# The first quarter's norm taken from channel-major tiles by products with ones, and the filler weights' split moved up

## The chip, the cores and the metric

The kernel runs on one core of one Trainium2 chip. The metric is the device time of one execution in microseconds (us). A core has a tensor engine (PE, with its weight loads as PEld), a vector engine (DVE), a scalar engine (ACT), a GpSimd engine (POOL) and a sync engine (SP), which here issues every DMA.

## The reference

One encoder block on 1024 tokens of 1024 channels, in float32:

```python
h = rms_norm(x, norm_mix_pre[l])      # x * rsqrt(mean(x*x over channels) + 1e-6) * g
proj = h @ w_in[l]                    # 1024 -> 5376 columns
p_sb, p_rw = ...                      # columns of attention and of RWKV-7
gates = sigmoid(proj[..., SB_COLS + RW_COLS:] + b_gate[l])
o_sb = stick_breaking_attention(q, k, v)
o_rw = rwkv7_time_mix(p_rw, ...)      # has a LoRA part and a chunked recurrence
merged = gates[..., :D] * (o_sb @ w_sb_out[l]) + gates[..., D:] * (o_rw @ w_rw_out[l])
x = x + rms_norm(merged @ w_o[l], norm_mix_post[l])
h = rms_norm(x, norm_ffn_pre[l])
x = x + rms_norm((silu(h @ w_ffn_gate[l]) * (h @ w_ffn_up[l])) @ w_ffn_down[l], norm_ffn_post[l])
```

The change touches the first line and the way in which some weight tiles of `gates` are prepared.

## The kernel before, in words

Every large product is done in three passes. A float32 operand is split into a high part (a cast on ACT) and a low part (a subtraction on DVE), and the products high by high, high by low and low by high are added in PSUM. `b.split` does this for any tile, `b.parts` for a weight tile of 128 x 1024, and `b.weights` is a load followed by `b.parts`. Loaded weights lie in the tile class `raw`, their parts in the classes `whi` and `wlo`; each of these classes has two places.

The kernel doesn't issue its instructions as they are written. `Block.record` writes down each operation with its cost, its tiles and a priority, which is its number in the order of writing plus an offset. `Block.schedule` then plays the whole program through with estimated durations and writes out an order for each engine: of the operations that are ready on an engine, the one with the lowest priority number goes first. It also hands out the places of the tile classes. So each engine's order is fixed when the kernel is built, from estimates, and nearly all instructions carry line 590, where the planned operations are issued. `with b.filler()` adds 10**7 to the priority: such work goes where nothing else is ready.

The stages in order of time are: the norm of x and the LoRA part (to about 63 us in the profile), four pairs of RWKV heads (`rwkv`, to about 440 us), the attention, the gates in pairs and the merge, the output projection, and the feed-forward part.

The first stage is `norm_in`. The tokens are worked in four quarters t of TQ = 256. x is loaded twice: token-major as `b.xin[m]` (eight tiles `b_x`, 128 tokens x 1024 channels, 512 KB each) and channel-major as `b.xt[2*t+q]` (eight tiles `b_xt`, 128 channels x 4 blocks x 256 tokens, 512 KB each). `scales(t)` takes the two token tiles of a quarter: ACT squares each and sums it along the row, ACT does Ln and Exp to have one over the root of the mean, DVE multiplies the identity by that number for each token (`b_dg`), and PE multiplies a tile of ones by this diagonal, so that the number of each token stands in all 128 partitions, in a PSUM tile (`e_e` for t = 0, 1 and `c_c` for t = 2, 3). Then for each of eight channel blocks DVE multiplies the channel-major tile by the channel's gain and by this row of scales (`SCALAR_TENSOR_TENSOR b_xt<-b_xt,par_par,e_e`, 128x256), and `b.split` writes the high and low parts into `b.hT` (`big_h`). `scales(t + 1)` is written down in the middle of quarter t.

`weights(i)` splits the two LoRA weight tiles (`b.w_lora`): the high part by a cast on POOL (`POOL CAST b_b<-raw_raw`), the low part by a subtraction on DVE (`TENSOR_TENSOR b_b<-raw_raw,b_b`). The LoRA products are the matmuls `d_d<-big_h,b_b` and `y_y<-big_h,b_b` of 256 columns, 192 of them.

The loads are issued by SP in the order written: token tile 0, the identity (`cst`), token tile 1, `par`, LoRA weight 0, the two channel tiles of t = 0, LoRA weight 1, token tiles 2 and 3, the channel tiles of t = 1, and so on.

`idle_products` are bf16 matmuls on zeros whose result nobody reads: nine at the start (`AWAKE[0]`), and eight (`AWAKE[1]`) that come after the last ones-product of the first quarter.

`gate_tiles` computes gate columns as filler: one weight tile is loaded and split, 48 matmuls of 512 columns follow in two halves of the tokens, ACT copies each half out of PSUM, and SP stores it (`gsc`). One such tile is written down in the first RWKV pair, one in the third, and two in the last part of the attention:

```python
GATES_R = (1, 0, 1, 0)
ATT_GATES = {(3, 0): 1, (3, 4): 1}
SINGLE = (8, 12, 9, 13)
```

Of the kernel before, what the change touches and what calls it, by code (L numbers as in the profile page):

```python
# [6 lines left out]
F32 = mybir.dt.float32  # L7
F32R = mybir.dt.float32r
BF16 = mybir.dt.bfloat16
AF = mybir.ActivationFunctionType  # L10
ALU = mybir.AluOpType
# [4 lines left out]
P = 128  # L16
S = 1024
D = 1024
KT = D // P
# [17 lines left out]
AWAKE = (9, 8)  # L37
TQ = S // 4
# [219 lines left out]
}  # L258
MARGIN = 80
CHAIN = -1000  # L260


def wait(e, to):
# [391 lines left out]
def hybrid_block(tc, x, xt, w_in, consts, params, rows, ups, gup, w_sb, w_rw, w_o, w_fg, w_fu, w_fd, out):  # L655
    b = Block(tc, {a.tensor.name for a in (x, xt, w_in, consts, params, rows, ups, gup, w_sb, w_rw, w_o, w_fg, w_fu, w_fd)})
    nc = b
    T = b.t
    with ExitStack() as es:
        b.open(es)  # L660
        b.cls("cst", 1, CC_TI)
        b.cls("par", 1, PC_N)
        b.cls("small", 4, 16)
        b.cls("tiny", 4, 4)
        b.cls("ss", 8, 4)
        b.cls("carry", 5, 1)
        b.cls("pl", 3, 8)
        b.cls("sp", 3, CH)
        b.cls("q", 4, 256)
        b.cls("big", 4, 4 * S)  # L670
        for n in ("raw", "whi", "wlo"):
            b.cls(n, 2, S)
        b.cls("b", NB, 1040, halves=True)
        for n, k in (("d", 2), ("e", 2), ("c", 2), ("y", 2)):
            b.cls(n, k, H, psum=True)

        cst, par = T("cst", [P, CC_TI]), T("par", [P, PC_N])

        one = T("q", [P, P])
        nc.gpsimd.memset(one, 1.0)  # L680
        b.zero = T("b", [P, H], BF16, "zero")
        nc.vector.memset(b.zero, 0.0)
        idle_products(b, AWAKE[0])

        b.xin, b.w_lora, b.xt = [], [], []
        def tokens(*ms):
            for m in ms:
                b.xin.append(T("b", [P, D], F32, "x"))
                nc.sync.dma_start(b.xin[m], x[m * P : m * P + P, :])
        def channels(t):  # L690
            for q in range(2):
                b.xt.append(T("b", [P, 4, TQ], F32, "xt"))
                nc.sync.dma_start(b.xt[-1], xt[t][:, 4 * q : 4 * q + 4, :])
        tokens(0)
        nc.sync.dma_start(cst[:, 0:P], consts[:, 0:P])
        tokens(1)
        nc.sync.dma_start(par, params)
        b.w_lora.append(b.load(w_in[24], [P, KT, P]))
        channels(0)
        b.w_lora.append(b.load(w_in[25], [P, KT, P]))  # L700
        tokens(2, 3)
        channels(1)
        tokens(4, 5)
        nc.sync.dma_start(cst[:, P:CC_TI], consts[:, P:CC_TI])
        channels(2)
        tokens(6, 7)
        channels(3)
        b.ident = cst[:, CC_ID : CC_ID + P]
        b.cen = cst[:, CC_CEN : CC_CEN + P]
        b.ones = cst[:, CC_ONE : CC_ONE + P]  # L710
        b.mask_a = cst[:, CC_MA : CC_MA + P]
        b.tinit = consts[:, CC_TI : CC_TI + 256]
        b.scanm = consts[:, CC_SC:CC_N]
        b.eps = T("small", [P, 2])
        nc.gpsimd.memset(b.eps[:, 0:1], RMS_EPS)
        nc.gpsimd.memset(b.eps[:, 1:2], GN_EPS)
        b.om = T("small", [P, 14])
        nc.gpsimd.tensor_scalar(out=b.om, in0=par[:, PC_MU : PC_MU + 14], scalar1=-1.0, scalar2=1.0, op0=ALU.mult, op1=ALU.add)
        b.oka = T("small", [P, 4])
        nc.gpsimd.tensor_scalar(out=b.oka, in0=par[:, PC_KA : PC_KA + 4], scalar1=-1.0, scalar2=1.0, op0=ALU.mult, op1=ALU.add)  # L720
        b.pc = lambda col: par[:, col : col + 1]

        b.gsc = [b.scratch([P, S], f"gsc{j}") for j in range(16)]
        b.orw_d = [b.scratch([P, S], f"orw{p}") for p in range(PAIRS)]
        b.x2_d = b.scratch([S, D], "x2d")
        b.w_in, b.w_sb, b.w_rw = w_in, w_sb, w_rw
        b.ngate = 0

        b.h_d = [b.scratch([4, P, S], f"h_d{q}") for q in range(2)]
        b.steady = STEADY[0]  # L730
        norm_in(b, one)
        lora(b, ups, gup)
        b.steady = STEADY[1]
        rwkv(b)
        b.steady = STEADY[2]
        attention(b)
        b.steady = STEADY[3]
        ms, sums = merge(b)
        b.steady = True
        output(b, x, w_o, rows, ms, sums)  # L740
        ffn(b, w_fg, w_fu, w_fd, rows, out)
        b.issue()


def idle_products(b, n, after=None):
    ps = b.t("y", [P, H])
    for i in range(n):
        b.tensor.matmul(ps, lhsT=b.zero[:, 0:P], rhs=b.zero, start=True, stop=True)
        if after:
            b.ops[-1].preds.add(after)  # L750


def norm_in(b, one):

    nc = b.nc
    T = b.t
    b.hT = tuple([T("big", [P, 4, S], F32R, "h") for q in range(2)] for i in range(2))
    b.table("natural_log_exp_and_others")
    ss = T("small", [P, 16])
    rs = []  # L760

    def scales(t):
        if t % 2 == 0:
            rs.append(T("ec"[t // 2], [P, 4, P]))
        dg = T("b", [P, 2, P], F32, "dg")
        for i in range(2):
            m = 2 * t + i
            nc.scalar.activation(b.xin[m], b.xin[m], AF.Square, accum_out=ss[:, m : m + 1])
        r = ss[:, 8 + 2 * t : 10 + 2 * t]
        nc.scalar.activation(r, ss[:, 2 * t : 2 * t + 2], AF.Ln, scale=1.0 / D, bias=b.eps[:, 0:1])  # L770
        nc.scalar.activation(r, r, AF.Exp, scale=-0.5)
        for i in range(2):
            nc.vector.tensor_scalar(out=dg[:, i], in0=b.ident, scalar1=r[:, i : i + 1], scalar2=None, op0=ALU.mult)
            nc.tensor.matmul(rs[t // 2][:, 2 * (t % 2) + i, :], lhsT=one, rhs=dg[:, i], start=True, stop=True)

    def weights(i):
        w = b.w_lora[i]
        hi, lo = T("b", [P, KT, P], F32R), T("b", [P, KT, P], F32R)
        nc.gpsimd.tensor_copy(hi, w)
        nc.vector.tensor_tensor(out=lo, in0=w, in1=hi, op=ALU.subtract)  # L780
        b.w_lora[i] = hi, lo

    scales(0)
    idle_products(b, AWAKE[1], b.ops[-1])
    weights(0)
    for t in range(4):
        r = rs[t // 2].rearrange("p i t -> p (i t)")[:, t % 2 * TQ : t % 2 * TQ + TQ]
        ts = slice(t * TQ, t * TQ + TQ)
        for q in range(2):
            h = b.xt[2 * t + q]  # L790
            for k in range(4):
                nc.vector.scalar_tensor_tensor(out=h[:, k], in0=h[:, k], scalar=b.pc(PC_G + 4 * q + k), in1=r, op0=ALU.mult, op1=ALU.mult)
                if k % 2:
                    ks = slice(k - 1, k + 1)
                    b.split(b.hT[0][q][:, ks, ts], b.hT[1][q][:, ks, ts], h[:, ks])
            with Offset(b, 500):
                nc.sync.dma_start(b.h_d[q][:, :, ts].rearrange("k p t -> p k t"), h)
            if t < 3 and q == 0:
                scales(t + 1)
            if t == 0 and q == 0:  # L800
                weights(1)


def gate_tiles(b, n):
    nc = b.nc
    with b.filler():
        for j in SINGLE[b.ngate : b.ngate + n]:
            w = b.weights(b.w_in[26 + j], [P, KT, P])
            for hf in range(2):
                ps = b.proj(w, hf)  # L810
                g = b.t("b", [P, H], F32, "g")
                nc.scalar.copy(g, ps)
                nc.sync.dma_start(b.gsc[j][:, hf * H : hf * H + H], g)
    b.ngate += n
# [173 lines left out]
def rwkv(b):  # L988
# [15 lines left out]
    for p in range(PAIRS):  # L1004
# [10 lines left out]
        if p == PAIRS - 1:  # L1015
            b.table("sigmoid_and_others")
        with Offset(b, CHAIN):
            for hf in range(2):
# [444 lines left out]
def output(b, x, w_o, rows, ms, sums):  # L1463
# [104 lines left out]
    product(Z, 3, True, False, third)  # L1568
    with Offset(b, CHAIN):
        for m in range(4):  # L1570
# [7 lines left out]
def ffn(b, w_fg, w_fu, w_fd, rows, out):  # L1578
    b.act = b.scratch([7, NFF // 2, P, H], "act")
    ffn_up(b, w_fg, w_fu)  # L1580
    ffn_down(b, w_fd, rows, out)
# [21 lines left out]
def ffn_up(b, w_fg, w_fu):  # L1603
# [38 lines left out]
    def first(r1, cls="d"):  # L1642
# [3 lines left out]
        e1 = T("b", [P, H], F32, "u")  # L1646
        with Offset(b, CHAIN):
            nc.scalar.copy(e1, pa)
# [4 lines left out]
    for g in range(LEAD):  # L1653
        e1, c11 = [], []
        for w in (w_fg, w_fu):
            e, pa = first(b.load(w[g], [P, KT, P]), "de"[w is w_fu])
            e1.append(e)
            c11.append(T("b", [P, H], F32, "u"))
            with Offset(b, CHAIN):
                nc.scalar.copy(c11[-1], pa)  # L1660
# [255 lines left out]
```

## Time and profile before

| | |
|---|---|
| median of three runs | 1575.42 us (1575.28 to 1575.59) |
| profiled execution, its own time | 1575.67 us |
| its span in the trace | 1573.9 us |
| PE busy | 1544.2 us, 98% of the span |
| PEld busy | 1248.3 us, 79% |
| DVE busy | 1201.3 us, 76% |
| ACT busy | 766.7 us, 49% |
| POOL busy | 203.7 us, 13% |
| DMA | 201.35 MB, mean 128 GB/s |

The span is counted from the first instruction of the trace. A row of the timeline reads: start, duration, engine, line, operation, out<-in, shapes, how many, and in brackets how long the engine was idle before it and what released it. In the table of stretches, each engine has its busy time and, in brackets, its instructions. A matmul's recorded duration is longer than its share of PE's time, because matmuls overlap.

### The profile page before, as it was taken

Reading aid. Unit: us, or ns where it says so; the run is one execution under the profiler, and the core shown is the slowest. Engines: PE = TensorE matmul, PEld = TensorE weight load, DVE = VectorE, ACT = ScalarE, POOL = GpSimd, SP = SyncE. Lnnn points to the kernel's source line nnn. Section 1 sums busy time; section 2 is a strip of 40 time slices with the busy share of each in tenths; the row PEclk is TensorE's granted clock in tenths of the full one; section 3 lists DMA queues with packets and bytes.
Section 4 is the critical chain, followed back from the end, with each engine's and each line's share of the span. In section 5 each row is a group of like instructions: output and inputs, shape, how many; then the busy total and the mean of one; then the engine's idle time right before and its main releaser. Section 6 shows DMA issues by size and latency. Waiting matters only on the chain.

```text
span 1573.9 us, 23740 instructions
## 1 busy us (share of the span) xinstructions
PE 1544.2 (98%) x8733; PEld 1248.3 (79%) x8733; DVE 1201.3 (76%) x2046; ACT 766.7 (49%) x1527; POOL 203.7 (13%) x383
## 2 busy tenths in 40 slices
PE   7999999999999999999999999999999999999998
PEld 6877777777887888788888887888888888888886
DVE  7769898987687979766379797778766766877575
ACT  6734453545577767523446696332323323454352
POOL 1132354444413220000000000000000000000000
PEclk9999999999999999999999999999999999999999
DMA  9723342322010003445632543334322323964543
GB/s 368 278 82 90 88 102 71 100 74 55 28 41 28 27 28 128 154 132 171 219 120 95 170 154 106 115 126 141 120 88 100 114 88 140 336 219 141 193 155 134
DMA packets 116949, 201.35 MB, mean 128 GB/s; under 512 B 43104, under 2 KB 48480, under 8 KB 116832
## 3 DMA queue, kind: packets, MB, share of 16 engines
q1 hardware_dynamic: 116832, 199.83, 38.0%
q8 instruction: 69, 1.13, 0.3%
q14 instruction: 48, 0.39, 0.1%
HBM read 146.05 MB, written 51.64 MB: 126 GB/s over the span
## 4 chain that ended last, share of the span: by engine, by line
PE 78%; DVE 10%; issue 3%; DMA 3%; ACT 3%; POOL 1%; SPq 0%; DVEq 0%; POOLq 0%; ACTq 0%
PE d_d L590 28%; PE e_e L590 20%; PE c_c L590 19%; PE y_y L590 12%; DVE q_q L590 1%; DVE b_sh L590 1%; DMA b_nl<-nd 1%; DVE b_nx L590 1%; DVE b_tmp L590 1%; POOL sp_sp L590 1%; ACT b_qst L590 1%; DVE b_nb L590 1%; DMA raw_raw<-w_fu 1%; DMA h_d<-b_xt 1%; DVE b_sv L590 1%
## 5 line engine op out<-in xcount | busy, mean ns | idle before, releaser
L590 PE MATMUL d_d<-big_h,whi_whi 128*128 128x512 f32 x896 | 308.7, 411 | 0.9 <-DVE b_sh L590 0.9
L590 PEld LDWEIGHTS d_d<-big_h,whi_whi 128*128 128x128 f32 x896 | 163.7, 189 | 33.3 <-issue 4.1
L590 PE MATMUL d_d<-big_h,wlo_wlo 128*128 128x512 f32 x448 | 184.9, 413 | 0.1
L590 PEld LDWEIGHTS d_d<-big_h,wlo_wlo 128*128 128x128 f32 x448 | 84.6, 189 | 16.2 <-issue 1.7
L590 DVE TENSOR_TENSOR_SCAN b_nb<-b_nb 128x128 f32<-128x128 f32 (+3 forms) x64 | 86.1, 1360 | 4.4 <-POOL b_nb L590 3.9
L590 POOL TENSOR_SCALAR sp_sp<-b_sv,pl_pl 64x64 f32<-64x64 f32 x120 | 66.8, 557 | 77.7 <-DVE b_sv L590 71.4
L590 ACT CAST whi_whi<-raw_raw 128x1024 fp32r<-128x1024 f32 (+1 forms) x44 | 39.2, 892 | 67.7 <-PE d_d L590 58.7
L590 PE MATMUL d_d<-b_wd,big_act 128*128 128x512 f32 x264 | 66.4, 394 | 0.0
L590 PE MATMUL e_e<-b_wd,big_act 128*128 128x512 f32 x264 | 66.3, 393 | 0.0
L590 PE MATMUL e_e<-big_h,whi_a 128*128 128x512 f32 x252 | 63.6, 395 | 0.0
L590 PE MATMUL e_e<-big_h,b_a 128*128 128x512 f32 x240 | 59.6, 394 | 0.0
L590 DVE TENSOR_TENSOR b_wd<-b_wraw,b_wd 128x512 fp32r<-128x512 f32 x65 | 42.5, 686 | 21.3 <-ACT b_wd L590 21.2
L590 PEld LDWEIGHTS d_d<-b_wd,big_act 128*128 128x128 f32 x264 | 49.6, 188 | 11.6
L590 PEld LDWEIGHTS e_e<-b_wd,big_act 128*128 128x128 f32 x264 | 49.6, 188 | 11.5
L590 PE MATMUL e_e<-big_h,wlo_a 128*128 128x512 f32 x228 | 56.3, 395 | 0.5 <-ACT b_mg L590 0.5
L590 ACT CAST b_wd<-b_wraw 128x512 fp32r<-128x512 f32 x65 | 38.6, 619 | 37.1 <-DVE b_wraw L590 14.5
L590 PEld LDWEIGHTS e_e<-big_h,whi_a 128*128 128x128 f32 x252 | 47.2, 188 | 11.0
L590 DVE TENSOR_TENSOR wlo_wlo<-raw_raw,whi_whi 128x1024 fp32r<-128x1024 f32 (+1 forms) x44 | 45.3, 1029 | 12.8 <-ACT whi_whi L590 12.7
L590 DVE TENSOR_TENSOR b_wt<-c_c,b_wt 128x512 fp32r<-128x512 f32 (+2 forms) x96 | 50.1, 546 | 4.6 <-ACT b_wt L590 3.9
L590 PEld LDWEIGHTS e_e<-big_h,b_a 128*128 128x128 f32 x240 | 45.1, 188 | 10.5
L590 PEld LDWEIGHTS e_e<-big_h,wlo_a 128*128 128x128 f32 x228 | 42.7, 188 | 11.0 <-ACT b_mg L590 1.0
L590 PE MATMUL d_d<-big_h,b_a 128*128 128x512 f32 x204 | 51.1, 395 | 0.1
(733 smaller groups left out, 3837.8 us busy)
## 6 DMA issues: line engine op xcount, KB each, us to landing
raw_raw<-w_in SPq DMA_DIRECT2D x48, 512.0 KB, 3.7
raw_raw<-w_fg SPq DMA_DIRECT2D x27, 512.0 KB, 3.5
raw_raw<-w_fu SPq DMA_DIRECT2D x27, 512.0 KB, 3.5
b_wraw<-w_fd SPq DMA_DIRECT2D x22, 512.0 KB, 5.2
act<-b_u SPq DMA_DIRECT2D x37, 256.0 KB, 2.2
b_x<-x SPq DMA_DIRECT2D x16, 512.0 KB, 5.8
b_mg<-gsc SPq DMA_DIRECT2D x30, 256.0 KB, 5.3
raw_araw<-act SPq DMA_DIRECT2D x14, 512.0 KB, 4.5
```

The costliest lines, as they stand in the source:

```text
L590: getattr(getattr(self.real, op.engine), op.method)(**kw)
```

## The change

Four things are done.

1. The loads of token tiles 0 and 1 are left out. The two channel-major tiles of t = 0 are loaded first, then `par`, LoRA weight 0, the identity, LoRA weight 1, and the rest as before.
2. For t = 0, `scales` gives way to `first_scales`. ACT squares the first channel-major tile, and four products by ones, of 256 columns in float32, add the squares over the 128 channels of a block. DVE squares the second tile, adds its halves, and two more products by ones follow into the same PSUM tile. Then ACT does Ln and Exp on 128 x 256 elements and writes the row of scales `r0` into SBUF, from where DVE's multiplications read it.
3. The eight idle products now come after the last of these six products.
4. In `gate_tiles`, the load keeps its filler priority, but the split of the weight tile is given the offset `SOON`, which takes the filler's 10**7 off again: the split competes by its place in the order of writing.

```diff
+SOON = -(10**7)
...
-        tokens(0)
-        nc.sync.dma_start(cst[:, 0:P], consts[:, 0:P])
-        tokens(1)
+        channels(0)
         nc.sync.dma_start(par, params)
         b.w_lora.append(b.load(w_in[24], [P, KT, P]))
-        channels(0)
+        nc.sync.dma_start(cst[:, 0:P], consts[:, 0:P])
         b.w_lora.append(b.load(w_in[25], [P, KT, P]))
         tokens(2, 3)
         channels(1)
...
     def scales(t):
-        if t % 2 == 0:
+        if t < 3:
             rs.append(T("ec"[t // 2], [P, 4, P]))
...
-    scales(0)
-    idle_products(b, AWAKE[1], b.ops[-1])
+    def first_scales():
+        ps = T("e", [P, TQ])
+        squares = [T("b", [P, 4, TQ], F32, "sq") for q in range(2)]
+        nc.scalar.activation(squares[0], b.xt[0], AF.Square)
+        for k in range(4):
+            nc.tensor.matmul(ps, lhsT=one, rhs=squares[0][:, k], start=k == 0, stop=False)
+        nc.vector.tensor_tensor(out=squares[1], in0=b.xt[1], in1=b.xt[1], op=ALU.mult)
+        nc.vector.tensor_tensor(out=squares[1][:, 0:2], in0=squares[1][:, 0:2], in1=squares[1][:, 2:4], op=ALU.add)
+        for k in range(2):
+            nc.tensor.matmul(ps, lhsT=one, rhs=squares[1][:, k], start=False, stop=k == 1)
+        r = T("b", [P, TQ], F32, "r0")
+        nc.scalar.activation(r, ps, AF.Ln, scale=1.0 / D, bias=b.eps[:, 0:1])
+        nc.scalar.activation(r, r, AF.Exp, scale=-0.5)
+        return r
+
+    r0 = first_scales()
+    idle_products(b, AWAKE[1], next(op for op in reversed(b.ops) if op.engine == "tensor"))
     weights(0)
     for t in range(4):
-        r = rs[t // 2].rearrange("p i t -> p (i t)")[:, t % 2 * TQ : t % 2 * TQ + TQ]
+        r = rs[t // 2].rearrange("p i t -> p (i t)")[:, t % 2 * TQ : t % 2 * TQ + TQ] if t else r0
...
         for j in SINGLE[b.ngate : b.ngate + n]:
-            w = b.weights(b.w_in[26 + j], [P, KT, P])
+            raw = b.load(b.w_in[26 + j], [P, KT, P])
+            with Offset(b, SOON):
+                w = b.parts(raw, [P, KT, P])
```

More of the change, by code (lines that the diff above doesn't have):

```diff
@@ L683, in hybrid_block @@
         idle_products(b, AWAKE[0])
-        b.xin, b.w_lora, b.xt = [], [], []
+        b.xin, b.w_lora, b.xt = {}, [], []
         def tokens(*ms):
             for m in ms:
-                b.xin.append(T("b", [P, D], F32, "x"))
+                b.xin[m] = T("b", [P, D], F32, "x")
                 nc.sync.dma_start(b.xin[m], x[m * P : m * P + P, :])
```

## The prediction

> **What bounds the kernel now.** I read the head of the page first, then a table of stretches of the whole run, which shows where PE stands still.
>
> ```profile
> span 1573.9 us, 23740 instructions
> PE 1544.2 (98%) x8733; PEld 1248.3 (79%) x8733; DVE 1201.3 (76%) x2046; ACT 766.7 (49%) x1527; POOL 203.7 (13%) x383
> ```
>
> ```profile
> 0.00:11.33 11.33, 5.25 (x14) 2.30 (x15) 1.53 (x3) 4.08 (x7) 2.90 (x12) 1.00 0.82 293
> 11.33:16.34 5.01, 3.62 (x10) 1.28 (x8) 5.01 (x9) 2.39 (x4) 1.04 (x1) 1.00 1.02 403
> 16.34:44.00 27.66, 26.59 (x206) 24.90 (x206) 25.97 (x54) 23.17 (x43) 1.79 (x7) 1.00 0.88 336
> 44.00:140.00 96.00, 95.97 (x465) 75.72 (x466) 70.36 (x120) 45.50 (x74) 18.75 (x44) 1.00 0.50 168
> 140.00:440.00 300.00, 290.79 (x2841) 227.71 (x2840) 257.80 (x596) 152.38 (x356) 135.31 (x249) 1.00 0.28 74
> 440.00:640.00 200.00, 198.22 (x1190) 169.06 (x1189) 174.49 (x256) 145.30 (x328) 43.87 (x70) 1.00 0.17 56
> 980.00:1560.00 580.00, 580.00 (x2506) 470.25 (x2505) 409.22 (x625) 211.99 (x353) 0.00 (x0) 1.00 0.43 148
> ```
>
> The columns are the stretch and its length, then busy time and instructions of PE, PEld, DVE, ACT and POOL, the granted clock, and the share and rate of the DMA. PE is the bound: it idles 29.7 us of 1573.9. What a change of order can gain is in those 29.7 us, because the change takes no product out of the later stages. They lie in three places that matter here: 7.5 us before 16.34 (6.08 + 1.39), 1.1 us from there to 44, and 9.2 us in the RWKV stretch from 140 to 440. The attention stretch has 1.8 us, and from 44 to 140 PE doesn't idle, so a head start gained by 44 is kept at least until 140.
>
> The third view is the timeline of the first stage. It shows that DVE is the feeder there.
>
> ```profile
> 4.05 1.06 ACT L590 ACTIVATE b_x<-b_x 128x1024 f32<-128x1024 f32 x1 [2.03 <-DMA b_x<-x]
> 7.08 1.06 ACT L590 ACTIVATE b_x<-b_x 128x1024 f32<-128x1024 f32 x1 [1.89 <-DMA b_x<-x]
> 8.90 1.25 DVE L590 TENSOR_SCALAR b_dg<-cst_cst,small_small 128x128 f32<-128x128 f32 x2 [7.76 <-ACT small_small L590]
> 10.10 1.19 PE L590 MATMUL e_e<-b_dg,q_q 128*128 128x128 f32 x4 [4.89 <-DVE b_dg L590]
> 11.09 3.36 PE L590 MATMUL y_y<-b_zero 128*128 128x512 bf16 x8
> 11.33 2.05 DVE L590 SCALAR_TENSOR_TENSOR b_xt<-b_xt,par_par,e_e 128x256 f32<-128x256 f32 x5 [1.18 <-PE e_e L590]
> 12.97 1.04 POOL L590 CAST b_b<-raw_raw 128x1024 fp32r<-128x1024 f32 x1 [3.10 <-DMA raw_raw<-w_in]
> 13.30 1.86 DVE L590 TENSOR_TENSOR big_h<-b_xt,big_h 128x512 fp32r<-128x512 f32 x2
> 15.08 1.21 DVE L590 TENSOR_TENSOR b_b<-raw_raw,b_b 128x1024 fp32r<-128x1024 f32 x1
> 16.34 4.02 PE L590 MATMUL d_d<-big_h,b_b 128*128 128x256 f32 x26 [1.35 <-DVE b_b L590]
> 20.20 0.61 PE L590 MATMUL e_e<-b_dg,q_q 128*128 128x128 f32 x4
> 20.85 2.83 DVE L590 SCALAR_TENSOR_TENSOR b_xt<-b_xt,par_par,e_e 128x256 f32<-128x256 f32 x7 [0.65 <-PE e_e L590]
> 27.93 2.05 DVE L590 SCALAR_TENSOR_TENSOR b_xt<-b_xt,par_par,c_c 128x256 f32<-128x256 f32 x5 [0.88 <-PE c_c L590]
> ```
>
> From 11.33, when the first scales arrive, DVE is busy without a break to 16.34 and for 25.97 of the 27.66 us after that. PE waits for it (1.35 us at 16.34, for the low part of the first LoRA weight). So the stage ends when DVE has worked off its list, and three things set that: when DVE may start (11.33), where it is held up, and the two waits of 0.65 and 0.88 us for the scales of the next quarters.
>
> **The change part by part, against the profiled execution's 1575.67 us** (span 1573.9 and 1.8 around it; it stands 0.25 us above the median of 1575.42).
>
> *Start of DVE's list.* Before, the second token tile let ACT start at 7.08, and the scales came to DVE at 11.33: 4.25 us later. Now the second channel tile stands where the second token tile stood, without the identity ahead of it. The first 512 KB landed by 4.05, as for a token tile. For the second I bound: not before 4.05 plus 512 KB at the 403 GB/s of the second stretch, 1.30 us, so 5.35; not after 7.08. I take 6.7, nearer to the row measured, since the LoRA weight that follows shares the engines as before. Then: DVE squares 128x1024, 1.21 us by the row at 15.08, to 7.9; DVE adds 128x512, and two products by ones follow. The normal DVE subtraction of 128x512, and the scalar engine on 128 x 256 out of PSUM, are in these rows (by tile, with shortest, median and longest; and by form, with the mean in ns behind the busy time):
>
> ```profile
> L590 DVE TENSOR_TENSOR big_h<-b_xt,big_h x16: 679/686/1255, 13.3 to 40.8; 128x512 fp32r<-128x512 f32 x16
> ```
>
> ```profile
> L590 ACT ACTIVATE b_nb<-e_e 128x256 f32<-128x256 f32 x16 | 6.3, 392 | 0.7 <-PE e_e L590 0.5
> ```
>
> The add takes 0.69, to 8.6. Two float32 products by ones of 128 columns took 0.61 us where PE had been busy (20.20) and 1.19 where it had idled for 4.89 us (10.10). With 256 columns I double: 1.2 or 2.4. PE's gap before them is here about 1.5 us (the first four products end near 7.1), nearer to no gap, so 1.2: to 9.8. Ln and Exp at 0.39 each: 10.55. DVE starts 0.8 us sooner. The ends: tile at 5.35 with fast products, 2.1 sooner; tile at 7.08 with slow products, 0.8 later. What is taken out here (ACT's two squares, two diagonals, two products) lay on this chain and is replaced whole; the first four new products and ACT's first square hide under the wait for the second tile.
>
> The Trainium skill ("TensorE: Matmul & The Clock Gate", What's actually happening) says that PE runs at half its clock by default and after an idle window of some 3.4 us, and at full clock after as long a busy one. The trace agrees that the early products are slow: the eight idle products of 512 columns took 3.36 us, 0.42 each, though the granted clock reads 1.00. By that rule the last two products run fast after a 1.5 us gap, and the sum stays; were the array still slow, it would be 1.2 us worse.
>
> *POOL beside DVE.* At 13.30 two subtractions took 1.86 where two cost 1.37; the longest of that kind, 1255 ns, lies beside POOL's cast of LoRA weight 1 at 12.97. That weight now has 1 MB less ahead of it, 2.6 us at 403 GB/s: the cast falls to about 10.4, on DVE's first multiplications. The gain of 0.5 is sure to move; I take back 0.2 for the new place: net -0.3, ends -0.5 (nothing is held) and +0.5 (a hold of the cast's whole 1.04).
>
> *Waits for the next scales.* Token tiles 2 and 3 come 2.6 us sooner by the same 1 MB. The scales of t = 1 then need not wait: I take the 0.65 out whole and, since ACT is busy 23.17 of 27.66 us by then, half of the 0.88: -1.1, ends 0 and -1.5. Late next is DVE itself.
>
> *Loads moved past others.* SP issues two loads fewer; `par` and the identity change places, and the identity is first needed by the diagonals of t = 1. Nothing: the cover is the work of quarter 0 on DVE. The eight idle products hold PE after the sum for 1.7 to 3.4 us, to at most 13.2, while the low part of LoRA weight 0 is not done before about 14: nothing.
>
> *The filler's split.* The gate weight of the first RWKV pair is one of the two casts below; its two halves leave at 145.23 and 163.40, and each cast waited for PE, that is for a place among the high parts.
>
> ```profile
> 125.67 1.07 ACT L590 CAST whi_whi<-raw_raw 128x1024 fp32r<-128x1024 f32 x1
> 135.82 1.04 ACT L590 CAST whi_whi<-raw_raw 128x1024 fp32r<-128x1024 f32 x1 [4.69 <-PE d_d L590]
> ```
>
> ```profile
> 145.23 0.34 SPq L590 DMA_DIRECT2D gsc<-b_tmp  x1
> 163.40 0.32 SPq L590 DMA_DIRECT2D gsc<-b_sh  x1
> ```
>
> ```profile
> L590 DVE TENSOR_TENSOR wlo_wlo<-raw_raw,whi_whi 128x1024 fp32r<-128x1024 f32 x14 | 17.2, 1226 | 1.5 <-ACT whi_whi L590 1.4
> L590 ACT CAST whi_whi<-raw_raw 128x1024 fp32r<-128x1024 f32 x14 | 14.7, 1047 | 19.0 <-PE d_d L590 19.0
> ```
>
> The last two rows are the 14 splits of the RWKV stretch: ACT idled 19.0 us in front of the casts for PE to free a place, not for priority. So a higher priority alone changes little: I take 0. The ends: a gain of a third of the 9.2 us that PE idles there, -3.1; a loss of one split's duration, 1.05 + 1.23 = 2.3, wherever a projection waits for a place that a filler weight holds.
>
> *A new order after the start.* All estimates behind the start shift, and the fixed orders may fall out otherwise with the same work. I take 0, ends 2 us on both sides, about a fifth of the idle time from 140 to 440.
>
> Sum: -0.8 - 0.3 - 1.1 + 0 + 0 = -2.2. From 1575.67 that is 1573.5, on the median 1573.3.
>
> **The rivals.**
>
> *The filler fills the RWKV waits* (faster). PE's longest waits in that stretch are for the chain on DVE:
>
> ```profile
> PE c_c L590 <- DVE b_sv L590: 2.2, 5, 0.8
> PE e_e L590 <- DVE b_nx L590: 1.9, 4, 0.7
> PE c_c L590 <- DVE b_xv L590: 1.8, 2, 1.2
> ```
>
> Ready gate products could fill them. Against it: the 19.0 us above, and that the row at 125.67 already lies before the first wait. With 3.1 us: 1570.2.
>
> *Given back* (same). DVE finishes sooner, but the RWKV chain, which waits for DVE and loads of its own, takes up the shift as longer PE waits. For it: 9.2 us idle in spite of filler. Against it: from 44 to 140 PE is full, so the shift does arrive. Time: 1575.4.
>
> *The cast on the multiplications* (less gained). `r0` is read from SBUF where PSUM was read before. At 12.97 the cast lay beside a multiplication with a PSUM operand and beside the subtraction, and it was the subtraction that got longer. If the multiplications are now held for the cast's 1.04 us, the sum loses 0.8: 1574.1. The Trainium skill ("GPSIMD Engine Reference", 1. Specifications) says that POOL shares its SBUF interfaces with DVE where DVE has two SBUF inputs. By that rule this hold comes. The trace agrees, with the 1255 ns.
>
> *A filler weight blocks a place* (slower). With two places, a gate weight that is split early and whose 48 products wait as filler leaves one place for the projections: each then costs a bare split of 2.3 us. Against it: during that time PE has just those filler products to do. It decides from three such stalls: 1573.3 + 6.9 = 1580.2.
>
> **How the numbers follow.** The forecast 1573.3 gets 0.46, with a range of its own of 1570.8 to 1575.5; the cast on the multiplications 0.08, given back 0.16, the filled waits 0.20, the blocked place 0.10. A measurement of this kernel can tell about 0.2% from no change: 3.15 us, so faster is below 1572.3 and slower above 1578.6. The filled waits are faster with 0.18, and 0.18 of the forecast's 0.46 lies below 1572.3: 0.36. Slower is the blocked place, 0.10. Same is the rest, 0.54. The range is 1568.8 to 1577.8: it leaves out most of the blocked place and the far tail of the filled waits.
>
> **What would show it.** Right: the first multiplication on DVE starts at 10.0 to 11.0; its list has no waits of 0.5 us for scales in quarter 1; PE's dense part starts before 15; the LoRA stage ends about 2 us sooner; PE's idle time from 140 to 440 stays within 2 us of 9.2. Wrong: the second channel tile lands after 7.1, the two last products by ones take over 2 us, or PE's idle time from 140 to 440 moves by more than the whole start gains. That last would make the time itself wrong.

## The result, and the profile after

The changed kernel takes 1564.17 us (median of 6 runs, 1563.44 to 1566.39), the one before 1575.09 (1573.91 to 1575.59): ratio 0.9934, interval 0.9922 to 0.9947. That is faster by 10.9 us; forecast were 2.2. The profiled execution took 1564.33 us with a span of 1562.5, against 1575.67 and 1573.9.

The head of the page after, and the table of stretches with the limits used before (stretch and length; busy time and instructions of PE, PEld, DVE, ACT, POOL; granted clock, DMA share and rate):

```profile
span 1562.5 us, 23763 instructions
PE 1539.6 (99%) x8741; PEld 1250.9 (80%) x8741; DVE 1204.9 (77%) x2046; ACT 765.7 (49%) x1524; POOL 209.5 (13%) x383
```

```profile
0.00:11.33 11.33, 8.26 (x29) 4.03 (x29) 3.36 (x6) 3.48 (x5) 5.25 (x13) 1.00 0.84 313
11.33:16.34 5.01, 2.67 (x12) 2.50 (x13) 5.01 (x12) 4.65 (x11) 0.00 (x0) 0.78 1.00 377
16.34:44.00 27.66, 27.66 (x212) 26.55 (x212) 27.46 (x54) 24.43 (x44) 1.84 (x6) 0.98 0.91 335
140.00:440.00 300.00, 290.79 (x2856) 230.26 (x2856) 259.21 (x591) 151.80 (x353) 137.73 (x251) 1.00 0.26 72
440.00:640.00 200.00, 199.50 (x1195) 171.18 (x1194) 180.21 (x266) 148.75 (x334) 45.96 (x68) 1.00 0.20 66
```

PE's idle time from 140 to 440 is 9.21 us, to the hundredth what it was. Yet PE ran 2856 products there in place of 2841. PE's busy column can't show that; the count of products can, and so can the busy time of the weight loads (227.71 us before, 230.26 after). The limits here are fixed and the changed kernel is some 3 us ahead, so the two stretches don't hold quite the same work; the table further down has its limits at events.

The timeline of the start after:

```profile
5.89 3.21 PE L591 MATMUL e_e<-b_sq,q_q 128*128 128x256 f32 x12 [1.26 <-ACT b_sq L591]
5.97 1.23 DVE L591 TENSOR_TENSOR b_sq<-b_xt 128x1024 f32<-128x1024 f32 x1 [4.83 <-DMA b_xt<-xt]
7.92 2.02 POOL L591 CAST b_b<-raw_raw 128x1024 fp32r<-128x1024 f32 x2
10.16 2.07 DVE L591 SCALAR_TENSOR_TENSOR b_xt<-b_xt,par_par,b_r 128x256 f32<-128x256 f32 x5 [2.24 <-ACT b_r L591]
13.29 1.28 DVE L591 TENSOR_TENSOR big_h<-b_xt,big_h 128x512 fp32r<-128x512 f32 x2
14.02 3.28 PE L591 MATMUL d_d<-big_h,b_b 128*128 128x256 f32 x14 [1.83 <-DVE big_h L591]
18.41 2.43 DVE L591 SCALAR_TENSOR_TENSOR b_xt<-b_xt,par_par,e_e 128x256 f32<-128x256 f32 x6
23.85 2.05 DVE L591 SCALAR_TENSOR_TENSOR b_xt<-b_xt,par_par,c_c 128x256 f32<-128x256 f32 x5
```

The second channel tile is there at 5.97, the first multiplication starts at 10.16 (before: 11.33). The two waits for scales (0.65 and 0.88) are both gone: the rows at 18.41 and 23.85 have no idle time in front. Both casts on POOL are over at 9.94, and two subtractions at 13.29 take 1.28 in place of 1.86.

For the rest, stretches are cut at the same events in each kernel: the first k-projection product (`d_d<-big_h,whi_whi`), the first and the last attention transpose (`c_c<-cst_cst,b_nb`), the first product of the paired gates with `b_tp`, and the first with `b_wd` (these two at their weight loads). The same columns, for the kernel before:

```profile
42.90:428.40 385.50, 376.21 (x3188) 293.98 (x3186) 319.75 (x701) 190.81 (x409) 151.84 (x288) 1.00 0.34 98
428.40:629.50 201.10, 199.32 (x1259) 170.22 (x1258) 173.62 (x254) 145.68 (x334) 46.09 (x75) 1.00 0.15 49
629.50:661.50 32.00, 30.27 (x140) 24.44 (x139) 27.16 (x45) 19.06 (x36) 0.00 (x0) 1.00 0.48 158
661.50:837.00 175.50, 175.50 (x757) 141.87 (x756) 109.75 (x171) 65.53 (x103) 0.00 (x0) 1.00 0.48 159
```

And for the changed kernel:

```profile
39.30:425.50 386.20, 376.99 (x3201) 296.93 (x3200) 322.91 (x702) 190.30 (x409) 150.73 (x289) 1.00 0.33 97
425.50:621.40 195.90, 195.41 (x1248) 168.53 (x1247) 172.96 (x253) 145.22 (x333) 51.66 (x75) 1.00 0.15 51
621.40:651.50 30.10, 30.10 (x140) 24.50 (x139) 27.13 (x45) 19.27 (x36) 0.00 (x0) 1.00 0.51 174
651.50:827.00 175.50, 175.50 (x757) 141.81 (x756) 110.48 (x172) 66.44 (x105) 0.00 (x0) 1.00 0.48 158
```

The first k-projection product comes 3.6 us sooner. The RWKV stretch is 0.7 longer, but holds 13 products more; the attention stretch is 5.2 shorter with 11 products fewer. By tile, the eleven are products of 512 columns with the split weights: with `whi_whi` there are 626 before and 634 after in the RWKV stretch, and 262 and 254 in the attention; with `wlo_wlo` 313 and 316, and 130 and 127. The other two are LoRA products that now lie behind the first k-projection product. Then 1.9 us go between 629.5 and 661.5, and nothing up to `b_wd`: 10.0 of the 11.4 us that the spans differ by lie ahead of the feed-forward part.

### The profile page after: what moved, and what is told of

It is laid out like the page before. It is cut to its first block, busy times and chain, and to the rows that moved or that the text cites. A ratio compares the mean times of both kernels' runs of the same rounds, so it can differ in the third digit from the quotient of the medians.

```text
span 1562.5 us, 23763 instructions
## 1 busy us (share of the span) xinstructions
PE 1539.6 (99%) x8741; PEld 1250.9 (80%) x8741; DVE 1204.9 (77%) x2046; ACT 765.7 (49%) x1524; POOL 209.5 (13%) x383
## 4 chain that ended last, share of the span: by engine, by line
PE 83%; DVE 10%; ACT 3%; DMA 2%; issue 1%; POOL 0%; SPq 0%; DVEq 0%; POOLq 0%; ACTq 0%
PE d_d L591 29%; PE e_e L591 22%; PE c_c L591 19%; PE y_y L591 13%; DVE q_q L591 2%; DVE b_tmp L591 1%; DVE b_sh L591 1%; DVE b_pp L591 1%; DVE b_sv L591 1%; DVE b_bk L591 1%; DVE b_nx L591 1%; ACT b_qst L591 1%; DMA q_q<-td 0%; DVE wlo_wlo L591 0%; DVE b_sg L591 0%
## 5 line engine op out<-in xcount | busy, mean ns | idle before, releaser
L591 PEld LDWEIGHTS e_e<-big_h,b_a 128*128 128x128 f32 x240 | 45.1, 188 | 10.4
```

The costliest lines, as they stand in the source:

```text
L591: getattr(getattr(self.real, op.engine), op.method)(**kw)
```

## The experiments

Three theories stood at the outset. *Head start*: what the start saves is carried to the end and is all there is. *Order*: an edit at the start changes every estimate behind it, the lists of all engines are dealt anew, and these lists are better. *Split first*: the new priority itself pays. Gains below are worked out from the ratio to the kernel before, timed beside each kernel, times 1575 us, with the 95% interval. The kernels are called by the first part of their names, `e1` to `e16`.

### The priority alone taken out, and one priority of four

`e1_norm_only` has the new norm and the old priority:

```diff
-            raw = b.load(b.w_in[26 + j], [P, KT, P])
-            with Offset(b, SOON):
-                w = b.parts(raw, [P, KT, P])
+            w = b.weights(b.w_in[26 + j], [P, KT, P])
```

> The changed kernel with the filler weights' split put back to its old priority; the new norm of the first quarter stays. The changed kernel took 1564.2 us and the one before 1575.1, so 10.9 us are to be explained. Theory 'head start' (the start is worth all of it, carried to the end): 1564 to 1565, and the split's priority is worth under 1 us. Theory 'order' (the start is worth the 3.5 us by which the first k-projection product comes sooner, the rest is the lists that fell out otherwise): the lists of this kernel are those of the changed one up to about 590 us and differ after that, so it should stand level with the changed kernel up to the last of the attention stretch and end anywhere from 1562 to 1572. Theory 'split first' (the priority itself pays): 1570 to 1572, the loss lying in the attention stretch.

`e9_last_split_first` gives it to the last weight alone:

```diff
-            with Offset(b, SOON):
+            with Offset(b, SOON if j == SINGLE[3] else 0):
```

> The changed kernel with the high priority for the split of the last filler gate weight alone (the one projected beside the last attention head); the three before it have the old priority. The lists come out instruction for instruction as the changed kernel's on all five engines, so this is also the changed kernel once more on this chip. Theory 'one split' (of the new priority only the last weight's matters): level with the changed kernel, 5 to 11 us below the kernel before, and 20 us and more below the kernel with the new norm alone. Rival 'all four matter': 3 us and more over the changed kernel. If start and order only add up, 1567 to 1570; if the changed kernel's first measurement holds on this chip, 1563 to 1566.

The first took 1589.83 us: 15.0 slower than before (12.4 to 17.3), outside what all three theories expected. The second took 1565.71, 10.2 faster (8.0 to 12.4), as the changed kernel, whose lists it has. So, given this norm, the priority of one split in four is worth 25 us; *split first* had the right stretch, with 6 to 8 us. With the old norm the same priority changes nothing: the lists come out as those of the kernel before, instruction for instruction.

The reason stands in the low parts of the filler weights on DVE, late in the attention stretch (view by tile from 555 us on: shortest, median, longest; first and last start). The kernel before, the changed one, and `e1_norm_only`:

```profile
L590 DVE TENSOR_TENSOR wlo_wlo<-raw_raw,whi_whi x2: 1190/1207/1224, 558.7 to 578.3; 128x1024 fp32r<-128x1024 f32 x2
```

```profile
L591 DVE TENSOR_TENSOR wlo_wlo<-raw_raw,whi_whi x1: 1209/1209/1209, 593.3 to 593.3; 128x1024 fp32r<-128x1024 f32 x1
```

```profile
L591 DVE TENSOR_TENSOR wlo_wlo<-raw_raw,whi_whi x1: 1219/1219/1219, 633.7 to 633.7; 128x1024 fp32r<-128x1024 f32 x1
```

With the old priority the last low part runs at 633.7, after the attention. Its 48 products, meant to fill PE's waits in the attention, then have no waits to fill, and PE stands still in both places. The timeline and the stretch of that kernel:

```profile
634.93 0.80 PE L591 MATMUL d_d<-big_h,wlo_wlo 128*128 128x512 f32 x1 [5.40 <-DVE wlo_wlo L591]
```

```profile
440.00:640.00 200.00, 186.18 (x1098) 158.71 (x1097) 177.76 (x262) 142.07 (x321) 46.14 (x69) 0.95 0.14 46
```

PE is idle for 13.8 us from 440 to 640, against 0.5 in the changed kernel, and the granted clock is 0.95 in place of 1.00.

### Start and order parted

`e2_new_norm_old_order` has the new norm and, from the LoRA products on, the kernel before's order on every engine and its places for the tiles, written out as lists; `e3_old_norm_new_order` is the converse; `e5_after_by_list` is the changed kernel with its own lists. The edit is the same in all:

```diff
-            for op in self.schedule():
+            for tile, at in zip(self.tiles, PLACES):
+                tile.where = (at // 2, at % 2, tile.small)
+            for op in (self.ops[k] for k in ORDER):
```

> The new norm of the first quarter, but from the LoRA projections on every engine runs its instructions in exactly the order of the kernel before, with every tile at the place that it had there (the order and the places are written out as a list). Theory 'head start': 1564 to 1566, since the start alone carries the gain. Theory 'order': 1571.0 to 1572.0, that is the 3.5 us that the first k-projection product came sooner and no more. Theory 'given back': 1574 to 1576.

> The converse: the old norm of the first quarter with its four token tiles, and from the LoRA projections on every engine's instructions in the order of the changed kernel, tiles at the changed kernel's places. Theory 'head start': 1574 to 1576, no gain. Theory 'order': 1567 to 1568.5, that is 7 to 7.5 us of gain with no sooner start. If both new_norm_old_order and this one gain less than their part, the order pays only together with the start.

> The changed kernel itself, its own order and places written out as a list: the same instructions in the same order on every engine. It is the measure for the kernels below and for the two mixed ones (new norm with old order: 3.3 us gained; old norm with new order: 2.7 us gained). If start and order add up and nothing else is at work, it stands about 6 us below the kernel before, at 0.996 of it; if the two pay only together, 10 to 11 us below, at 0.993, as the changed kernel did.

They gained 3.3 us (1.7 to 4.7), 2.5 (1.1 to 3.8) and 5.5 (3.5 to 7.7); the last was timed on another chip than the first two. So neither part carries the whole, and the three were run once more side by side:

> The changed kernel's order as a list, beside the two mixed kernels on one chip. It gained 5.8 us on one chip, and the changed kernel itself 9.5 on the other, on which the mixed ones gained 3.3 and 2.7. Theory 'start and order add up': its gain here is that of the two mixed kernels together, within 1.5 us. Theory 'they pay only together': its gain is larger than their sum by 3 us or more.

> The new norm with the order of the kernel before, beside the other two on one chip. Theory 'start and order add up': 2.8 to 3.5 us under the kernel before, by the 2.8 us that the first k-projection product came sooner in its profile. Theory 'they pay only together': the same, but the three don't sum.

> The old norm with the changed kernel's order, beside the other two on one chip. In its first profile it stood 5.2 us ahead at the FFN's first weight and lost 2 after that, at a granted clock of 0.97 from 920 to 980 us. Theory 'start and order add up', with the order worth 5: 5 us under the kernel before. Theory 'they pay only together': 2.7 us again.

Now 8.2 (6.1 to 10.2) for both, 3.5 (2.2 to 4.9) for the new norm alone and 3.3 (1.9 to 4.9) for the new order alone. 3.5 + 3.3 = 6.8 lies inside the first interval: start and order add up as well as this can be told, with 1.4 us left over that the intervals don't settle. Each is worth about as much as the other. *Head start* as the whole cause is out, *order* is right in kind. The stretches show what each does. New norm, old order (`e15`):

```profile
40.20:425.70 385.50, 375.79 (x3187) 294.11 (x3186) 319.15 (x701) 190.34 (x408) 150.78 (x288) 1.00 0.33 97
425.70:626.60 200.90, 199.05 (x1260) 170.16 (x1260) 173.56 (x254) 145.71 (x334) 46.33 (x75) 1.00 0.15 49
```

Old norm, new order (`e16`):

```profile
43.40:429.10 385.70, 378.11 (x3202) 296.70 (x3200) 323.20 (x701) 190.24 (x409) 150.89 (x289) 1.00 0.34 98
429.10:625.10 196.00, 195.57 (x1247) 168.34 (x1245) 172.82 (x252) 145.26 (x333) 51.78 (x75) 1.00 0.15 51
```

The norm moves the stretches and leaves them as long as before. The order moves 13 or so products from the attention, where PE idles 1.8 us in 201, into the RWKV stretch, which takes them at no visible cost of time (385.5 to 386.2 us in these four profiles, with 3187 or with 3202 products). One execution differs from another by more than that: in the profile of `e14`, with the changed kernel's lists, the stretch took 388.6 us. The attention is then 5 us shorter: 13 products at 0.23 us (2506 in 580 us in the row of the last stage before) are 3.0, less idle time is 1.4 (1.85 to 0.43), and 0.5 us is not accounted for.

Why do 5 us in the attention show as 3.3 in the time of `e16`? The timeline at the entry of the feed-forward part shows where some of it goes. The kernel before, the changed one, and `e16`:

```profile
950.39 3.05 PE L590 MATMUL d_d<-big_h,whi_a 128*128 128x512 f32 x12 [1.27 <-ACT b_mg L590]
```

```profile
939.99 3.02 PE L591 MATMUL d_d<-big_h,whi_a 128*128 128x512 f32 x12 [1.17 <-ACT b_t L591]
935.41 0.62 ACT L591 CAST b_a<-raw_raw 128x512 fp32r<-128x512 f32 x1 [0.82 <-DMA raw_raw<-w_fu]
```

```profile
947.29 4.61 PE L599 MATMUL d_d<-big_h,whi_a 128*128 128x512 f32 x12 [2.59 <-ACT b_t L599]
942.72 0.62 ACT L599 CAST b_a<-raw_raw 128x512 fp32r<-128x512 f32 x1 [2.25 <-DMA raw_raw<-w_fu]
```

In `e16` ACT waits 2.25 us for a load of `w_fu` in place of 0.82, PE waits 2.59 in place of 1.17, and the 12 products behind it take 4.61 in place of 3.02: 1.4 + 1.6 = 3.0 us. The execution profiled is a long one (1574.14 us against the median of 1570.88), so this may be more than an execution at the median lost. `e3`, profiled near its median (1572.52 and 1572.14), has the same (2.14 us idle, then 4.53): 1.0 + 1.5 = 2.5 us. In `e16` the load took 6.6 us from its issue at 936.15 to the cast, in the changed kernel 5.1 (from 930.30); why was not tried.

### The start made later, and its loads put back

`e6_start_late` issues ACT's first square four times; `e7_loads_kept` loads the two token tiles and does not use them. Both run in the changed kernel's lists and stand beside `e5` (1568.23).

```diff
-        nc.scalar.activation(squares[0], b.xt[0], AF.Square)
+        for i in range(4):
+            nc.scalar.activation(squares[0], b.xt[0], AF.Square)
```

> The changed kernel with the scalar engine's first square (1.06 us) issued four times into the same tile, so that the first multiplication starts some 2 to 3 us later (the second tile's square on the vector engine hides about 1 us); everything else in the changed kernel's order. Theory 'the start is carried one to one': 2 to 3.5 us over the changed kernel. Theory 'given back' (the chain further on takes the shift up): under 1 us. Theory 'the order fits this start alone' (start and order pay only together): 5 us and more, that is as much as the two lost when they were parted.

```diff
         b.w_lora.append(b.load(w_in[25], [P, KT, P]))
+        tokens(0, 1)
         tokens(2, 3)
```

> The changed kernel with the two token tiles of the first quarter (1 MB) loaded all the same, behind the second LoRA weight, and not used; everything else in the changed kernel's order. The token and channel tiles behind them come some 2.6 us later. Theory 'the waits for the scales went because 1 MB less lies ahead': the waits of 0.65 and 0.88 us in front of the multiplications come back and the first k-projection product starts 1 to 2.6 us later; 1 to 2.5 us over the changed kernel. Theory 'DVE's own list is what sets the stage': no wait comes back, under 0.5 us.

`e6` took 1571.66 us, 3.4 more. Its start was later than meant:

```profile
9.18 4.63 PE L600 MATMUL e_e<-b_sq,q_q 128*128 128x256 f32 x12 [3.97 <-ACT b_sq L600]
15.76 1.67 DVE L600 SCALAR_TENSOR_TENSOR b_xt<-b_xt,par_par,b_r 128x256 f32<-128x256 f32 x4 [5.50 <-ACT b_r L600]
```

The first multiplication came 5.6 us after that of `e5` (10.16), because PE had idled 3.97 us and its products then took 4.63. By the first starts in the view by tile, 5.2 of these are left at the first k-projection product (44.8 against 39.6), 4.5 at the first `b_wd` product (832.7 against 828.2), and 3.4 in the medians. So most of a shift of the start is carried, though not all of it; *given back* is out, and an order that fits one start alone would have lost more.

`e7` took 1566.3 us, not slower than `e5`. The tile of the next quarter came 1 us later than in the changed kernel (11.60), not 2.6, and no wait came back:

```profile
12.56 1.06 ACT L600 ACTIVATE b_x<-b_x 128x1024 f32<-128x1024 f32 x1 [0.96 <-DMA b_x<-x]
18.78 2.43 DVE L600 SCALAR_TENSOR_TENSOR b_xt<-b_xt,par_par,e_e 128x256 f32<-128x256 f32 x6
24.11 2.04 DVE L600 SCALAR_TENSOR_TENSOR b_xt<-b_xt,par_par,c_c 128x256 f32<-128x256 f32 x5
```

So the megabyte was not why the waits went. By the rows it was ACT's list, though no run changed that list alone. Before, the first square of t = 1 began when its tile came, at 14.20, and the second stood behind a cast that waited for DVE:

```profile
16.71 0.62 ACT L590 CAST big_h<-b_xt 128x512 fp32r<-128x512 f32 x1 [1.37 <-DVE b_xt L590]
17.24 1.05 ACT L590 ACTIVATE b_x<-b_x 128x1024 f32<-128x1024 f32 x1
```

After, the cast between the two squares doesn't wait, and both are done by 14.2:

```profile
11.60 1.05 ACT L591 ACTIVATE b_x<-b_x 128x1024 f32<-128x1024 f32 x1
13.16 1.05 ACT L591 ACTIVATE b_x<-b_x 128x1024 f32<-128x1024 f32 x1
```

In `e15`, which has the new start and the old order from the LoRA products on, the first wait is gone too, and 0.34 us of the second is left.

### The same work in other lists

One number of the estimates is changed; no instruction is added or removed.

```diff
-MARGIN = 80
+MARGIN = 90
```

> The kernel before with one number of its estimates changed, the allowance for a wait between engines, from 80 to 90: no instruction is added or removed, only the lists of the engines fall out otherwise (some 590 of 2046 places on the vector engine, 2680 of 7649 products). Theory 'order': the time moves by 2 to 8 us in one of the two directions, so a re-dealt order alone can make the size that is unexplained. Theory 'head start': within 1.5 us of 1575.1, since the same work at the same start takes the same time.

> The changed kernel with the one number of its estimates, the allowance for a wait between engines, at 90 in place of 80: the same instructions, the lists fall out otherwise (some 780 of 2046 places on the vector engine, 3320 of 7653 products). Theory 'order' (the changed kernel's lists happen to be good ones): 3 to 8 us over the changed kernel, that is at 1567 to 1572, where the sooner start alone would leave it. Theory 'head start': within 1.5 us of the changed kernel.

And with 70:

> The kernel before with the allowance for a wait between engines at 70 in place of 80: the same instructions, the lists fall out otherwise. Theory 'order': a time several us off the kernel before, in either direction. Theory 'head start': within 1.5 us of it, as with 90.

> The changed kernel with the same allowance at 70: the same instructions, the lists fall out otherwise. Theory 'order': 3 us and more over the changed kernel (at 90 it was 15.8 over). Theory 'head start': within 1.5 us of it.

The kernel before moved by +0.8 (-0.8 to 2.2) and +29.8 (27.6 to 31.8); the changed one stood 9.5 over the kernel before (7.6 to 11.5) and level with it (+1.3, -0.5 to 2.8), that is 15.0 us over `e5` and 11.5 over `e9`, the changed kernel's lists timed beside each. Lists alone thus span 30 us. In `e8` the loss lies in the RWKV stretch: 42.4 to 440.9 by first starts, 398.5 us against 386.2. In `e10` it is the late split again:

```profile
L590 DVE TENSOR_TENSOR wlo_wlo<-raw_raw,whi_whi x2: 1222/1224/1225, 558.2 to 645.6; 128x1024 fp32r<-128x1024 f32 x2
```

`e13_before_70_split_first` is `e10` with the new priority, the same edit as in the change:

> The kernel before with the allowance at 70, which took 1605.0 us, and now the high priority for the filler weights' split as in the changed kernel; old norm, the same instructions. In the profile of the 1605 us the low part of the last filler weight ran 65 us after its high part, and its products came after the attention stretch. Theory 'the late split made the loss': 25 us and more go away, to 1574 to 1580. Rival 'the lists were bad all over': 5 us or less go away, to 1600 or more.

```profile
L591 DVE TENSOR_TENSOR wlo_wlo<-raw_raw,whi_whi x2: 1208/1216/1225, 554.4 to 600.5; 128x1024 fp32r<-128x1024 f32 x2
```

It took 1578.03 us, 27 less. So the late split made that loss, and the priority mends it with either norm; where the lists have no late split, it does nothing.

### A version meant to beat both

`e12_shared_square` keeps the changed kernel's lists, lets ACT square half of the second channel tile and adds three idle products.

```diff
-AWAKE = (9, 8)
+AWAKE = (12, 8)
...
-        nc.vector.tensor_tensor(out=squares[1], in0=b.xt[1], in1=b.xt[1], op=ALU.mult)
+        nc.scalar.activation(squares[1][:, 0:2], b.xt[1][:, 0:2], AF.Square)
+        nc.vector.tensor_tensor(out=squares[1][:, 2:4], in0=b.xt[1][:, 2:4], in1=b.xt[1][:, 2:4], op=ALU.mult)
```

> The changed kernel in its own order with two edits at the start: the scalar engine squares half of the second channel tile beside the vector engine's half, and three more idle products keep the array busy up to the products by ones. By the row of 1.23 us for 128x1024 and 0.69 for 128x512, the sum stands 0.5 us sooner; where the products by ones run slow (4.8 us in place of 3.2 in one profile) the idle products save up to 1.6 more. Theory 'the start is carried one to one': 0.5 to 1.5 us below the changed kernel. Theory 'given back': level with it.

```profile
9.68 2.07 DVE L600 SCALAR_TENSOR_TENSOR b_xt<-b_xt,par_par,b_r 128x256 f32<-128x256 f32 x5 [2.29 <-ACT b_r L600]
```

The first multiplication starts 0.5 us sooner, as worked out. The time, 1566.6 us (ratio 0.9940, 0.9928 to 0.9953), can't be told from that of `e9`, timed beside it (0.9935). It beats the kernel before and is level with the changed one.

## Why the prediction was wrong, point by point

The direction was right; the size was not, and the time lies below the range. The forecast fell 8.7 us short: the first three terms below make up 1.1 of these, the new order by itself 3.3, and the remaining 4.3 stay without a term of their own (see *What stays open*).

*Start of DVE's list.* Forecast 0.8 us sooner, measured 1.17. The term that was off is the landing of the second tile: 6.7 assumed, 5.97 measured. (The first came at 4.69, not 4.05, which stayed hidden behind the second.) The products by ones were done at 9.10 (5.89 + 3.21), against 9.8; Ln and Exp with the waits around them took 1.06 in place of 0.78. The slow array, which the working named, does happen: see the last section.

*POOL beside DVE.* Forecast 0.3, measured 0.58 (1.86 - 1.28). The casts fell from 7.92 to 9.94, while DVE was idle (the 2.24 us in the row at 10.16), and not on the multiplications. So the rival of the cast on the multiplications had no place to happen.

*Waits for the next scales.* Forecast 1.1, measured 1.53. The size is near; the reason given, 1 MB less on the way, is wrong by `e7`. What went, by the rows, was ACT's square behind a waiting cast.

These three make 3.3 us, not 2.2, and agree with 3.6 at the first k-projection product and with the 3.3 and 3.5 us that the new norm gained under the old order (where that product came 2.8 and 2.7 us sooner).

*"A new order after the start. ... I take 0, ends 2 us on both sides."* This is the step that failed. The order alone was worth 3.3 us by time and 5 in the attention stretch. The bounds came from PE's idle time (a fifth of 9.2 us), but a RWKV stretch of 385 us took 13 more products with its idle time unchanged (9.29 and 9.21 us): its room lies in time that counts as busy. The heads of the two pages say so of the whole kernel. PE's idle time fell by 6.8 us (29.7 to 22.9) and its busy time by 4.6, with 8 recorded products more, while the prediction looked for gains in the 29.7 us alone. Whether that room is gaps too short to count or products recorded longer than they need was not measured. And the bound on the other side was too small by far, since other lists of the same work cost up to 30 us.

*The filler's split.* The prediction took 0 for it, by the 19.0 us that ACT waited for places. It looked at the RWKV stretch and at the high parts. What decided was the low part of one weight in the attention stretch: 25 us between `e1` and `e9`. That the 0 did no harm was luck of the lists: in the old ones the split isn't late, and in the new ones the changed priority keeps it early, without which the new norm would have cost 15.0 us. The mechanism wasn't among the rivals.

*The rivals.* Given back: out, by `e6`. The filler fills the RWKV waits: right in kind (more products with split weights in that stretch), but by way of the lists and without filling the waits, which stayed 9.2 us in sum: that for `b_nx` fell from 1.9 to 0.2 us, that for `b_xv` rose from 1.8 to 3.3. A filler weight blocks a place: not seen (ACT's idle time in front of the casts fell from 19.0 to 9.6 us from 140 to 440); the opposite, a filler weight that comes too late, is what costs.

*What would show it.* The first multiplication at 10.16, no waits for scales, PE's dense part from 14.02, idle time from 140 to 440 unchanged: all as written, and the time was wrong all the same. For the later stages, the list of signs watched idle time only.

*What stays open.* Start and order by themselves make 6.8 us; the changed kernel's lists with its norm made, by ratio, 10.4, 10.2, 8.2 and 5.5 in four measurements. In profiles the attention's 5.2, the start's 3.6 and 1.9 between 629.5 and 661.5, less the 0.7 by which the RWKV stretch is longer, make the 10. The idle time in that last stretch (1.7 us before) was 0.3 and 0.8 in the two profiles with the new norm alone and 0.8 and 1.6 with the new order alone; what sets it was not tried.

## What to carry to other kernels

Where one planner deals the order of all engines, a local edit has two prices: its own, and that of the new lists. The first can be worked out from rows; the second can be larger and of either sign, so measure it with the lists held fixed, and see with a changed estimate how far lists alone scatter. Count products between like events, since the idle time of the bounding engine doesn't show all the room that there is. And follow the last piece of filler: both halves of its operand must be ready while there are still waits to fill.

## What the runs showed of the hardware that was not expected

The same products by ones (six, recorded as twelve) after the same nine idle ones took 3.2 us in some profiles and 4.65 to 4.80 in others: of ten with this start seven were done by 9.2 us and three (`e8`, `e9`, `e14`) at 10.55 to 10.71. It isn't the program that decides: `e14` runs the instructions of `e5`, and `e9` those of the changed kernel, in the same order. One of the slow ones, the timeline of `e9`:

```profile
5.90 4.65 PE L591 MATMUL e_e<-b_sq,q_q 128*128 128x256 f32 x12 [0.68 <-ACT b_sq L591]
11.61 2.07 DVE L591 SCALAR_TENSOR_TENSOR b_xt<-b_xt,par_par,b_r 128x256 f32<-128x256 f32 x5 [3.50 <-ACT b_r L591]
```

The first multiplication comes 1.45 us later than in the changed kernel's profile, at the same work. And PE lost speed after short idle times late in the kernel: 12 products took 4.53 and 4.61 us after 2.14 and 2.59 us of idling (`e3` and `e16`, with a granted clock of 0.68 and 0.64 from 947.3 to 952), and 3.02 to 3.08 after 0.5 to 1.3. The Trainium skill ("TensorE: Matmul & The Clock Gate", What's actually happening) has a half clock after an idle window of some 3.4 us that runs freely and isn't reset by the kernel. A free-running window would fit the seven and three, but no run here tests it. The 2.14 and 2.59 us of idling that were enough in two profiles are less than the figure, and there the measurement stands.
